# A hybrid decoder layer on one core: VectorE's other work behind the score masks, GpSimd scaling in halves, block stores in the order of their read

## The chip, the cores and the metric

The kernel runs on one core of one Trainium2 chip. The metric is the device time of one execution in microseconds (us), as the median of several runs. A profile of one execution comes from the hardware profiler.

## The reference

One inference step of a decoder layer with d = 1024, for one prompt of 512 tokens and eight sample requests of 4 tokens each, which share all weights (so 544 columns per matmul row block). A SwiGLU feed-forward part (half a step), a layer norm, then a mixer, a layer norm, a second feed-forward part and a last norm. Only the mixer is touched here:

```python
proj = x @ p["w_in"]                       # 1024 -> 3328
ps_mix = ps + p["mu_shift"] * (prev - ps)  # token shift, gives r, k, v, wd, ad, gd
o, wkv_new = wkv7_recurrence(r_h, w_h, k_h, v_h, kk, a_h, wkv0)
#   S <- S diag(w) + (S (-kk)) (kk*a)^T + v k^T ;  o = S r      per head, per token
u = c_c * c_h
z = cw[0] * u_full[:, 0:T] + cw[1] * ... + cw[2] * ...
y_conv = c_b * z
mix = jnp.concatenate([y_rwkv, y_conv], axis=-1) @ p["w_out"]
```

Half of the mixer is the recurrence of 8 heads of 64, the other half a short convolution of three taps over 512 channels, with a gate before and behind it.

## The kernel before

**Weights.** Matmuls run on a split format: ScalarE writes the high half of a weight (L147), VectorE the rest, the low half (L148, 128x1024 a time). Weights come through a ring of `raw` tiles and a ring of `hl` tiles (`ring`, L109 to L115); a `raw` tile is loaded by SP's queue and is free again when both halves are made. `mm3` (L159) does three matmuls per block: high by high, high by low part of the input, low by high. Only the third reads the low half. It yields after every six.

**Order.** A scheduler lists the instructions of each engine; while `pinned[0]` is set, TensorE's follow the program. `bg` is a queue of generators with background work (projections and convolutions); `take(ns)` draws so many nanoseconds of it into the program, `need(p, n)` draws until pair p is that far. `tc.issue_after(ins)` puts whatever is emitted under it behind `ins` in the order list, on its engine.

**The recurrence.** The 512 tokens are cut into 8 chunks of 64, and the sample's tokens make a ninth (index 8). Heads go in four pairs (`Pair`, L884 to L988), one head on each half of the partitions. For each pair: gates, squares and decays, `prep` (VectorE multiplies keys and queries by decay products, L931 to L944), then `scores`, where TensorE runs pinned. `masked(0, 4)` and `masked(4, 4)` make the products AO of chunks 0 to 7, and VectorE multiplies them by masks into SC (L955, four times 128x512). Two DMAs per pair store the parts of SC that the elimination needs to `Ad` in DRAM, GpSimd scales `bkb` (L962), and at `yield 1` the main loop puts in `FILL["s"]` = 600 ns of background work, which is one step of a convolution: six matmuls. Then `masked(8, 1)` for the sample, the transposes of `vt` and `bkb`, whose results ScalarE moves to UV (L977) and BK (L984), and the `Pn` products (L988). A PSUM pool `sm` has 5 banks, `big` (tile name `mm`) 3. After the scores of pair p, the rest of pair p + 1 (`own_b`: decays, prep, the vt projection) is drawn.

**Convolutions.** `conv` (L810) makes c, then h (multiplied to u), then the taps on VectorE (L806), then the gate, one tile `zc` for all of it.

**After the pairs.** `elim` (L992) reads `Ad` to AT, inverts all 32x32 triangles in 31 pairs of VectorE steps (L1006, L1008), stores the result De and its transpose to `Dd`, reads them as DM and XT, and joins the blocks in two rounds of small matmuls, with copies of XT on VectorE and ScalarE (L1036). `sample` (L1127) treats the ninth chunk while `elim` runs. `chain` (L1049) goes through the chunks one after another: `values` makes W (L1066), `solve` multiplies by XT, then `update` and `outputs`.

Of the kernel before, what the change touches and what calls it, by code (L numbers as in the profile page):

```python
# [62 lines left out]
def body(ctx: ExitStack, tc: tile.TileContext, xT, gu1, wd1, win, wo_c, wo_r, gu2, wd2, lora, vec, cst,  # L63
# [746 lines left out]
    def conv(i):  # L810
        u = cvp.tile([P, 2 + TP + 6 * NSEQ], F32, name="cu")
        zc = cvp.tile([P, T], F32, name="zc")
        us = u[:, 514:].rearrange("p (b t) -> p b t", t=6)
# [65 lines left out]
    POOL.memset(cm[:, 512:576:4], 0.0)  # L879
    Ad = dr.tile([2, 32, 65, 64], F32, name="Ad")  # L880
    Dd = [dr.tile([2, 32, 2, 32, 32], F32, name=f"Dd{i}") for i in range(2)]
    SEG = ((0, 256, 0), (256, 576, 1))

    class Pair:  # L884
# [61 lines left out]
        def scores(self):  # L946
            p, bkb, vf = self.p, self.bkb, vfs[self.p]
            def masked(a0c, n):
                qs = (sm(), sm())
                for c in range(n):  # L950
                    for par, q in enumerate(qs):
                        PE.matmul(q[:, c * P:c * P + P], bkb[R(par), a0c + c, :, :],
                                  AO[R(par), 0:p + 2:p + 1, a0c + c, :] if n > 1 else AR8[R(par), p, :, :], start=True, stop=True)
                for par, q in enumerate(qs):
                    DVE.tensor_tensor(SC[:, p, par, a0c:a0c + n, :], q[:, :P * n].rearrange("p (c t) -> p c t", c=n),  # L955
                                      (msk if n > 1 else msks)[:, None, :].to_broadcast([P, n, P]), op=OP.mult)

            masked(0, 4)
            masked(4, 4)
            for par in range(2):  # L960
                dma(Ad[par].rearrange("(c d) s t -> d s c t", d=4)[p, 0:64], SC[R(par), p, par, 0:8, 0:64])
            POOL.tensor_tensor(bkb[:, 0:8], bkb[:, 0:8], Pe[:, p, :, None, None].to_broadcast([P, 8, 2, 64]), op=OP.mult)  # L962
            yield 1
            masked(8, 1)
            for a0c, n in ((0, 5), (5, 4)):
                qs = (big(), sm())
# [25 lines left out]
    def elim(XT, DM):  # L992
# [4 lines left out]
        tm = ep.tile([P, 256], F32, name="tm")  # L997
        dma(AT, bass.AP(tensor=Ad.tensor, offset=Ad.offset, ap=[[2080, P], [64, 32], [1, 32]]))
        POOL.memset(De, 0.0)
# [49 lines left out]
    def chain(XT, tl):  # L1049
# [10 lines left out]
        def values(g, c):  # L1060
            q = sm()
            for pl, par in PP:
                p, r = 2 * g + pl, slice(0, P) if c else R(1 - par)
                PE.matmul(q[R(par), pl * 64:pl * 64 + 64], SC[r, p, par, c, 0:64], UV[r, p, par, c, :], start=True, stop=True)
            W[g] = tl([P, 2, 64], F32, name=f"W{g}")
            ACT.activation(W[g], v2(q), AF.Copy)  # L1066
# [35 lines left out]
        def outputs(g, c):  # L1102
# [3 lines left out]
            if c % 4 == 3:  # L1106
                ACT.activation(O[:, 2 * g:2 * g + 2, c - 3:c + 1, :],
                               qo[g].rearrange("p (c d t) -> p d c t", c=4, d=2), AF.Copy)

        for c in range(8):  # L1110
            if c % 4 == 0:
                qo[:] = big(), big()
            values(0, c)
            if c:
                reads(0, c)
            values(1, c)
            solve(0, c)
            if c:
                reads(1, c)
            solve(1, c)  # L1120
            yield 0
            for g in range(2):
                update(g, c)
                outputs(g, c)
            yield 0

    def sample(cp):  # L1127
        tl = cp.tile
        S0 = tl([P, 4, NSEQ, 64], F32, name="S0")
        dma(S0, s0)  # L1130
        WT = tl([P, 4, 32], F32, name="WT")
        SI = tl([P, 4, 2, 64], F32, name="SI")
        D8 = tl([P, 4, 32], F32, name="D8")
        X8 = tl([P, 4, 64], F32, name="X8")
        UP = tl([P, 4, 64], F32, name="UP")
        HR = [slice(96 * par, 96 * par + 32) for par in range(2)]
# [19 lines left out]
        for rnd in range(3):  # L1156
# [12 lines left out]
            reads(rnd)  # L1169
            yield 0  # L1170
        reads(3)
        for par in range(2):
            pr = R(par)
# [5 lines left out]
        for pl, par in PLP:  # L1179
            PE.matmul(q[R(par), pl * 64:pl * 64 + 64], SC[:, pl, par, 8, 0:64], SI[:, pl, par, :], start=True, stop=True)  # L1180
        W = tl([P, 4, 64], F32, name="W")
        ACT.activation(W, v4(q), AF.Copy)
# [4 lines left out]
        DVE.tensor_copy(UV[R(0), :, 0, 8, :], v4(q[0], R(0)))  # L1187
        ACT.copy(UV[R(1), :, 1, 8, :], v4(q[1], R(1)))
        DVE.tensor_tensor(UP, UV[:, :, 0, 8, :], UV[:, :, 1, 8, :], op=OP.add)
        uxs = [tl([P, NSEQ, 64], F32, name="ux", bufs=4) for _ in range(4)]  # L1190
# [77 lines left out]
    POOL.tensor_copy(T12[:, T:576], T12[:, 512:T])  # L1268
    ACT.activation(sgd, sgd, AF.Sigmoid)
    pairs[0].gates()  # L1270
    pairs[0].square()
    wget(4)
    wget(5)
    pairs[0].decays()
    pairs[0].prep()
    drain(project(4, 8, 0, vfs[0]), project(4, 8, 1, vfs[0]))
    bg.append(convs)
    for p in range(4):
# [6 lines left out]
        for _ in pairs[p].scores():  # L1285
            take(FILL["s"])
        pinned[0] = False
        if p < 3:
            bg.appendleft(own_b(p + 1))
            need(p + 1, 2)  # L1290
            take(FILL["p0"])
    pst.close()
# [25 lines left out]
    next(el)  # L1318
    drain(conv3)
    for _ in el:  # L1320
        pass
# [11 lines left out]
    cst0 = ExitStack()  # L1333
    cp = pool(cst0, "chain")
    for _ in chain(XT, cp.tile):
        pass
# [48 lines left out]

    f2.s1[0] = s1
    f2.open()
    lnq = f2.open_lnq()
# [87 lines left out]
```

## Time and profile before

| what | value |
|---|---|
| median of three runs | 1082.21 us (1079.39 to 1083.17) |
| the profiled execution | 1080.19 us, its span in the profile 1078.4 us |
| TensorE busy | 1054.3 us, 98% of the span |
| VectorE busy | 833.0 us, 77% |
| ScalarE busy | 564.3 us, 52% |
| GpSimd busy | 206.4 us, 19% |
| TensorE's granted clock, mean | 0.991 |

PE is TensorE's matmuls, DVE is VectorE, ACT is ScalarE, POOL is GpSimd, SP the engine that issues most DMAs. In a timeline a bracket tells how long the engine sat idle before the instruction and what released it. A granted clock of 1.00 is 2.4 GHz, 0.50 is 1.2 GHz. The mixer's pairs lie at about 405 to 530 us, elimination and sample at 530 to 598, the chain from there to about 626.

### The profile page before, as it was taken

Reading aid. Unit: us, or ns where it says so; the run is one execution under the profiler, and the core shown is the slowest. Engines: PE = TensorE matmul, PEld = TensorE weight load, DVE = VectorE, ACT = ScalarE, POOL = GpSimd, SP = SyncE. Lnnn points to the kernel's source line nnn. Section 1 sums busy time; section 2 is a strip of 40 time slices with the busy share of each in tenths; the row PEclk is TensorE's granted clock in tenths of the full one; section 3 lists DMA queues with packets and bytes.
Section 4 is the critical chain, followed back from the end, with each engine's and each line's share of the span. In section 5 each row is a group of like instructions: output and inputs, shape, how many; then the busy total and the mean of one; then the engine's idle time right before and its main releaser. Section 6 shows DMA issues by size and latency. Waiting matters only on the chain.

```text
span 1078.4 us, 22059 instructions
## 1 busy us (share of the span) xinstructions
PE 1054.3 (98%) x8960; PEld 1021.0 (95%) x8960; DVE 833.0 (77%) x1528; ACT 564.3 (52%) x1015; POOL 206.4 (19%) x296
## 2 busy tenths in 40 slices
PE   9999999999999999999999999999999999999996
PEld 8999999999999998888989899999999999999995
DVE  7798888889775857787588578878889888887755
ACT  6655565555552567555312464466554655545524
POOL 0122230312200023343220410010313122130000
PEclk9999999999999999999989999999999999999998
DMA  8568595866854231222616631424957759496302
GB/s 295 129 125 191 124 216 134 177 158 145 197 122 147 77 116 40 69 52 87 153 59 200 237 104 40 138 59 89 213 145 164 178 125 225 105 211 138 104 1 84
DMA packets 82887, 144.78 MB, mean 134 GB/s; under 512 B 20448, under 2 KB 44384, under 8 KB 82528
## 3 DMA queue, kind: packets, MB, share of 16 engines
q1 hardware_dynamic: 55584, 107.19, 30.7%
q0 software_dynamic: 27200, 36.18, 21.7%
q8 instruction: 70, 1.15, 0.4%
q14 instruction: 33, 0.27, 0.1%
HBM read 124.37 MB, written 10.06 MB: 125 GB/s over the span
## 4 chain that ended last, share of the span: by engine, by line
PE 79%; DVE 9%; DMA 6%; ACT 3%; issue 2%; SPq 0%; POOL 0%; ACTq 0%; DVEq 0%; POOLq 0%
PE mm L76 50%; PE sm L76 29%; DVE hl L148 2%; DMA z<-sv 2%; DMA z<-cpb 1%; ACT hl L147 1%; DVE De L1008 1%; DMA raw<-in_gu 1%; DVE SC L955 1%; DVE tm L1006 1%; DVE hhl L152 1%; DMA raw<-in_wd 1%; DMA DM<-Dd 1%; DMA z<-in_xT 0%; DVE z L610 0%
## 5 line engine op out<-in xcount | busy, mean ns | idle before, releaser
L76 PE MATMUL mm<-xhl,hl 128*128 128x288 f32 (+2 forms) x2640 | 362.8, 293 | 3.5 <-DVE hl L148 2.3
L76 PEld LDWEIGHTS mm<-xhl,hl 128*128 128x128 f32 x2640 | 343.6, 189 | 11.2 <-DVE hl L148 2.5
L148 DVE TENSOR_TENSOR hl<-raw,hl 128x1024 fp32r<-128x1024 f32 (+3 forms) x224 | 262.0, 1175 | 69.1 <-ACT hl L147 68.3
L147 ACT ACTIVATE hl<-raw 128x1024 fp32r<-128x1024 f32 (+3 forms) x224 | 224.4, 1012 | 91.6 <-DVE raw L487 31.3
L76 PE MATMUL sm<-xhl,hl 128*128 128x272 f32 (+1 forms) x1392 | 193.8, 289 | 0.3 <-DVE xhl L152 0.3
L76 PEld LDWEIGHTS sm<-xhl,hl 128*128 128x128 f32 x1392 | 182.3, 189 | 1.5 <-ACT xhl L151 0.6
L76 PE MATMUL mm<-tv,hl 128*128 128x272 f32 x864 | 121.3, 289 | 1.9 <-ACT cpb L587 1.8
L76 PE MATMUL mm<-hhl,hl 128*128 128x272 f32 (+2 forms) x792 | 119.2, 294 | 0.1
L76 PEld LDWEIGHTS mm<-tv,hl 128*128 128x128 f32 x864 | 113.3, 188 | 3.0 <-ACT cpb L587 2.3
L76 PEld LDWEIGHTS mm<-hhl,hl 128*128 128x128 f32 x792 | 105.9, 188 | 5.1 <-ACT sv L626 1.5
L76 PE MATMUL sm<-hhl,hl 128*128 128x272 f32 (+2 forms) x792 | 109.6, 288 | 0.0
L76 PEld LDWEIGHTS sm<-hhl,hl 128*128 128x128 f32 x792 | 103.0, 188 | 0.5
L493 POOL DMA_DIRECT2D raw<-in_gu x36 | 43.5, 1209 | 256.2 <-DVE cpb L583 81.4
L499 POOL DMA_DIRECT2D raw<-in_wd x32 | 39.3, 1469 | 269.2 <-DVE hlb L152 235.6
L76 PE MATMUL mm<-tv,hlb 128*128 128x272 f32 x432 | 61.1, 291 | 0.8 <-ACT cpb L590 0.8
L76 PEld LDWEIGHTS mm<-tv,hlb 128*128 128x128 f32 x432 | 56.4, 188 | 2.3 <-ACT cpb L590 2.2
L151 ACT ACTIVATE hhl<-sv 128x272 fp32r<-128x272 f32 (+1 forms) x52 | 26.0, 512 | 30.8 <-DVE sv L350 12.1
L152 DVE TENSOR_TENSOR hlb<-raw,hlb 128x512 fp32r<-128x512 f32 x52 | 35.7, 687 | 4.2 <-ACT hlb L151 4.2
L151 ACT ACTIVATE hhl<-hk 128x272 fp32r<-128x272 f32 (+1 forms) x48 | 24.2, 504 | 27.5 <-DVE hk L557 12.9
L218 ACT ACTIVATE lnq<-z 128x512 f32<-128x512 f32 (+1 forms) x24 | 14.9, 654 | 41.5 <-DVE z L217 41.5
L487 DVE TENSOR_TENSOR raw<-raw 128x512 f32<-128x512 f32 x52 | 35.8, 689 | 1.0
L76 PE MATMUL mm<-hhl,hlb 128*128 128x272 f32 (+2 forms) x264 | 36.4, 288 | 0.0
(294 smaller groups left out, 1325.9 us busy)
## 6 DMA issues: line engine op xcount, KB each, us to landing
raw<-in_gu SPq DMA_DIRECT2D x84, 512.0 KB, 4.6
raw<-in_gu POOLq DMA_DIRECT2D x36, 512.0 KB, 6.2
raw<-in_wd SPq DMA_DIRECT2D x32, 512.0 KB, 4.7
raw<-in_win SPq DMA_DIRECT2D x26, 512.0 KB, 3.6
raw<-in_wd POOLq DMA_DIRECT2D x32, 256.0 KB, 6.0
raw<-in_wd SPq DMA_DIRECT2D x16, 384.0 KB, 3.1
z<-cpb POOLq DMA_DIRECT2D x16, 272.0 KB, 9.0
z<-sv POOLq DMA_DIRECT2D x16, 272.0 KB, 7.3
```

The lines of the kernel that those rows point to most:

```text
L76: ins = f(*args, **kw)
L147: ACT.activation(hl[:, 0, a:b], raw[:, a:b], AF.Copy)
L148: DVE.tensor_tensor(hl[:, 1, a:b], raw[:, a:b], hl[:, 0, a:b].bitcast(F32), op=OP.subtract)
L151: ACT.activation(hi, x, AF.Copy)
L152: DVE.tensor_tensor(lo, x, hi.bitcast(F32), op=OP.subtract)
L218: sq = ACT.activation(qq, zz, AF.Square)
L487: DVE.tensor_tensor(y[:, :, 0], y[:, :, 1], a[:, :, 1], op=OP.add)
L493: POOL.dma_start(x.rearrange("p (s c) -> p s c", s=2), bass.AP(tensor=a11.tensor, offset=a11.offset, ap=[[2 * D, P], [P * 2 * D, 2], [1, 5 ...
L499: POOL.dma_start(four(x)[:, i], bass.AP(tensor=a11.tensor, offset=a11.offset, ap=[[DFF, P], [P * DFF, 2], [1, 256]]), accum_op=OP.add)
L955: DVE.tensor_tensor(SC[:, p, par, a0c:a0c + n, :], q[:, :P * n].rearrange("p (c t) -> p c t", c=n), (msk if n > 1 else msks)[:, None, :].t ...
L1006: DVE.tensor_tensor(tv, AT[:, k, k + 1:32, None].to_broadcast([P, n, k + 1]), De[:, k, None, 0:k + 1].to_broadcast([P, n, k + 1]), op=OP.mult)
L1008: DVE.tensor_tensor(De[:, k + 1:32, 0:k + 1], De[:, k + 1:32, 0:k + 1], tv, op=OP.add)
```

## The change

It does eight things, all between the first projections of the mixer and the start of the chain:

- In the main loop, all background work that is drawn during and after a pair's scores stands behind `pairs[p].mk`, the last mask emitted so far (at `yield 1` the fourth).
- GpSimd scales `bkb` in two halves, each right after its four chunks; the second bank of `masked(8, 1)` comes from `big`, and the transposes go in groups of 4 and 5 chunks rather than 5 and 4.
- `Ad` is laid out as the blocks that the elimination reads: four stores of 32x8x32 in place of two of 64x8x64 for each pair, and a contiguous read.
- `zc` gets two buffers.
- Two weights are fetched ahead of pair 0's gates, and four steps of the convolutions and one more fetch run ahead of pair 0's vt projection.
- `values(0, 0)` and `values(1, 0)` of the chain are emitted ahead of the last rounds of `elim`; W of chunk 0 uses AR8's space.
- `sample` uses two tile names for two purposes each, and asks for 600 ns of filler in its second and third round.
- The counter of the `raw` ring is set to 0 ahead of the second feed-forward part.

```diff
-        zc = cvp.tile([P, T], F32, name="zc")
+        zc = cvp.tile([P, T], F32, name="zc", bufs=2)
...
-    Ad = dr.tile([2, 32, 65, 64], F32, name="Ad")
+    Ad = dr.tile([2, 32, 2, 32, 32], F32, name="Ad")
...
             def masked(a0c, n):
-                qs = (sm(), sm())
+                qs = (sm(), sm() if n > 1 else big())
...
-                    DVE.tensor_tensor(SC[:, p, par, a0c:a0c + n, :], q[:, :P * n].rearrange("p (c t) -> p c t", c=n),
+                    self.mk = DVE.tensor_tensor(SC[:, p, par, a0c:a0c + n, :], q[:, :P * n].rearrange("p (c t) -> p c t", c=n),
...
-            masked(0, 4)
-            masked(4, 4)
+            for c in (0, 4):
+                masked(c, 4)
+                POOL.tensor_tensor(bkb[:, c:c + 4], bkb[:, c:c + 4], Pv[:, c:c + 4].to_broadcast([P, 4, 2, 64]), op=OP.mult)
             for par in range(2):
-                dma(Ad[par].rearrange("(c d) s t -> d s c t", d=4)[p, 0:64], SC[R(par), p, par, 0:8, 0:64])
-            POOL.tensor_tensor(bkb[:, 0:8], bkb[:, 0:8], Pe[:, p, :, None, None].to_broadcast([P, 8, 2, 64]), op=OP.mult)
+                for b in range(2):
+                    dma(Ad[par, :, b].rearrange("(c d) s t -> d s c t", d=4)[p],
+                        SC[64 * par + 32 * b:64 * par + 32 * b + 32, p, par, 0:8, 32 * b:32 * b + 32])
             yield 1
             masked(8, 1)
-            for a0c, n in ((0, 5), (5, 4)):
+            for a0c, n in ((0, 4), (4, 5)):
...
-        dma(AT, bass.AP(tensor=Ad.tensor, offset=Ad.offset, ap=[[2080, P], [64, 32], [1, 32]]))
+        dma(AT, Ad.rearrange("a c b s t -> (a c b) s t"))
...
-            W[g] = tl([P, 2, 64], F32, name=f"W{g}")
+            W[g] = tl([P, 2, 64], F32, name=f"W{g}") if c else AR8[:, g]
...
+        values(0, 0)
+        values(1, 0)
+        yield 0
...
+    wget(4)
+    wget(5)
     pairs[0].gates()
     pairs[0].square()
-    wget(4)
-    wget(5)
     pairs[0].decays()
     pairs[0].prep()
+    drain(islice(convs, 4))
+    wget(6)
     drain(project(4, 8, 0, vfs[0]), project(4, 8, 1, vfs[0]))
...
         for _ in pairs[p].scores():
-            take(FILL["s"])
+            with tc.issue_after(pairs[p].mk.ins):
+                take(FILL["s"])
         pinned[0] = False
         if p < 3:
             bg.appendleft(own_b(p + 1))
-            need(p + 1, 2)
-            take(FILL["p0"])
+            with tc.issue_after(pairs[p].mk.ins):
+                need(p + 1, 2)
+                take(FILL["p0"])
...
     drain(conv3)
+    cpool = [None]
+    ch = chain(XT, lambda *a, **k: cpool[0].tile(*a, **k))
+    next(ch)
     for _ in el:
         pass
```

What this does to the order is seen at three places, all in pair 1. First VectorE from the end of pair 1's projections through its masks. `SC` lines are masks, `zc` lines of L806 the taps of convolution 0, `hl_` lines low halves of weights, `kq`, `AO` and `AR8` lines pair 2's prep. Before:

```order
L938 TENSOR_TENSOR AO_4712<-r_4313,Pi_5553 128x512
L939 TENSOR_TENSOR AR8_4713<-r_4313,Pi_5553 128x64
L148 TENSOR_TENSOR hl_5678<-raw_5677,hl_5678 128x1024
L955 TENSOR_TENSOR SC_4719<-sm_5456,cs_4710 128x512
L955 TENSOR_TENSOR SC_4719<-sm_5457,cs_4710 128x512
L955 TENSOR_TENSOR SC_4719<-sm_5468,cs_4710 128x512
L955 TENSOR_TENSOR SC_4719<-sm_5469,cs_4710 128x512
L955 TENSOR_TENSOR SC_4719<-sm_5489,cs_4710 128x128
L955 TENSOR_TENSOR SC_4719<-sm_5490,cs_4710 128x128
L932 SCALAR_TENSOR_TENSOR AO_4712<-kq_5404,Pi_5553 128x512
L936 TENSOR_TENSOR kq_5404<-kq_5404,a_5279 128x576
```

And now:

```order
L957 TENSOR_TENSOR SC_4719<-sm_5479,cs_4710 128x512
L957 TENSOR_TENSOR SC_4719<-sm_5480,cs_4710 128x512
L957 TENSOR_TENSOR SC_4719<-sm_5492,cs_4710 128x512
L957 TENSOR_TENSOR SC_4719<-sm_5493,cs_4710 128x512
L806 SCALAR_TENSOR_TENSOR zc_4506<-cu_4505,vc_66,zc_4506 128x512
L806 SCALAR_TENSOR_TENSOR zc_4506<-cu_4505,vc_66,zc_4506 128x32
L806 SCALAR_TENSOR_TENSOR zc_4506<-cu_4505,vc_66,zc_4506 128x512
L806 SCALAR_TENSOR_TENSOR zc_4506<-cu_4505,vc_66,zc_4506 128x32
L148 TENSOR_TENSOR hl_5518<-raw_5517,hl_5518 128x1024
L957 TENSOR_TENSOR SC_4719<-sm_5529,cs_4710 128x128
L957 TENSOR_TENSOR SC_4719<-mm_5530,cs_4710 128x128
L931 SCALAR_TENSOR_TENSOR kq_5426<-k0_4314,vc_66,kq_5426 128x576
```

The two lines of prep and the split that stood ahead of the masks have gone behind them, and between the fourth mask and the two narrow ones there are now the taps and one split.

TensorE at the same place, from the end of the AO products: the fill of six matmuls (`xhl` by a weight), chunk 8 (`AR8`) and the first transposes. Before:

```order
L76 MATMUL sm_5469<-AO_4712,bkb_5144 128x128
L76 MATMUL mm_5449<-xhl_68,hl_5248 128x288 x6
L76 MATMUL sm_5489<-AR8_4713,bkb_5144 128x128
L76 MATMUL sm_5490<-AR8_4713,bkb_5144 128x128
```

And now:

```order
L76 MATMUL sm_5493<-AO_4712,bkb_5178 128x128
L76 MATMUL mm_5522<-xhl_68,hl_5518 128x256 x6
L76 MATMUL sm_5529<-AR8_4713,bkb_5178 128x128
L76 MATMUL mm_5530<-AR8_4713,bkb_5178 128x128
L76 MATMUL mm_5535<-cs_4710,vt_4297 64x64
```

The fill was the middle of a product whose weight hl_5248 had been in use for 30 matmuls; now it is the first use of hl_5518, whose low half is the ninth line of VectorE's list above.

ScalarE now, from the tap that it does itself to the first evictions of pair 1 (`UV` and `BK`):

```order
L147 ACTIVATE hl_5622<-raw_5621 128x1024
L804 ACTIVATE zc_4506<-cu_4505,vc_66 128x512
L804 ACTIVATE zc_4506<-cu_4505,vc_66 128x32
L981 ACTIVATE UV_4721<-mm_5535 64x256
L981 ACTIVATE UV_4721<-sm_5536 64x256
L147 ACTIVATE hl_5749<-raw_5748 128x1024
L988 ACTIVATE BK_4720<-sm_5547 128x4x64
L988 ACTIVATE BK_4720<-sm_5548 128x4x64
L981 ACTIVATE UV_4721<-mm_5559 64x320
L981 ACTIVATE UV_4721<-sm_5560 64x320
L988 ACTIVATE BK_4720<-sm_5573 128x5x64
```

Before, no split stood among pair 1's evictions; now the one of hl_5749 stands between the first of UV and the first of BK.

## Rows read from the trace of the kernel before

**Rows 1.** The page: busy time by engine, and DMA issues (median us to landing).
```profile
PE 1054.3 (98%) x8960; PEld 1021.0 (95%) x8960; DVE 833.0 (77%) x1528; ACT 564.3 (52%) x1015; POOL 206.4 (19%) x296
...
raw<-in_win SPq DMA_DIRECT2D x26, 512.0 KB, 3.6
```

**Rows 2.** Windows, the four pairs: us; busy of PE, PEld, DVE, ACT, POOL; PEclk, DMA.
```profile
400.00:540.00 140.00, 134.32 (x1164) 124.14 (x1164) 97.23 (x181) 80.02 (x165) 50.17 (x111) 0.99 0.29 83
```

**Rows 3.** PE's timeline in pair 0: start, us, instruction, [idle before, releaser].
```profile
424.27 2.86 PE L76 MATMUL mm<-xhl,hl 128*128 128x256 f32 x22 [2.32 <-DVE hl L148]
...
434.15 1.06 PE L76 MATMUL mm<-xhl,hl 128*128 128x288 f32 x6
...
436.07 0.49 PE L76 MATMUL sm<-AR,bkb 64*128 64x128 f32 x2 [0.45 <-DVE SC L955]
...
440.77 1.24 PE L76 MATMUL sm<-Pn,cs 128*128 128x256 f32 x4 [0.82 <-ACT BK L984]
441.60 1.11 PE L76 MATMUL mm<-xhl,hl 128*128 128x256 f32 x6
```

**Rows 4.** PE's timeline in pair 1: fill, first BK transpose, next projection.
```profile
468.21 1.06 PE L76 MATMUL mm<-xhl,hl 128*128 128x288 f32 x6
...
471.41 0.24 PE L76 MATMUL sm<-cs,bkb 64*128 64x64 f32 x1 [0.15 <-DVE SC L955]
...
473.74 1.46 PE L76 MATMUL mm<-xhl,hl 128*128 128x256 f32 x9
```

**Rows 5.** DVE's timeline: pair 1's split and masks, convolution taps, pair 3's split.
```profile
468.24 1.22 DVE L148 TENSOR_TENSOR hl<-raw,hl 128x1024 fp32r<-128x1024 f32 x1
469.38 2.88 DVE L955 TENSOR_TENSOR SC<-sm,cs 128x512 f32<-128x512 f32 x6
...
484.87 1.73 DVE L806 SCALAR_TENSOR_TENSOR zc<-cu,vc,zc 128x512 f32<-128x512 f32 x4
...
524.28 1.23 DVE L148 TENSOR_TENSOR hl<-raw,hl 128x1024 fp32r<-128x1024 f32 x1 [3.66 <-ACT hl L147]
```

**Rows 6.** Groups by line and form, DVE, 405 to 530: busy us, mean ns.
```profile
L936 DVE TENSOR_TENSOR kq<-kq,a 128x576 f32<-128x576 f32 x4 | 3.4, 849 | 0.1
...
L955 DVE TENSOR_TENSOR SC<-sm,cs 128x128 f32<-128x128 f32 x8 | 1.9, 281 | 0.0
...
L939 DVE TENSOR_TENSOR AR<-r,Pi 128x64 f32<-128x64 f32 x4 | 0.9, 218 | 0.0
```

**Rows 7.** ACT's timeline: a split, BK evictions in pair 1, W of the chain.
```profile
466.34 1.07 ACT L147 ACTIVATE hl<-raw 128x1024 fp32r<-128x1024 f32 x1
...
472.42 0.77 ACT L984 ACTIVATE BK<-sm 128x320 f32<-128x320 f32 x2 [0.24 <-PE sm L76]
...
598.78 0.45 ACT L1066 ACTIVATE W<-sm 128x128 f32<-128x128 f32 x2
```

**Rows 8.** Windows with a low clock (columns as in rows 2).
```profile
504.00:510.00 6.00, 5.59 (x51) 4.58 (x52) 5.56 (x11) 3.61 (x9) 2.86 (x3) 0.72 0.52 134
542.00:550.00 8.00, 8.00 (x106) 7.66 (x104) 3.77 (x14) 0.59 (x3) 0.00 (x0) 0.57 0.01 2
```

**Rows 9.** POOL's timeline: the scaling of bkb in pairs 1 and 3.
```profile
468.40 2.82 POOL L962 TENSOR_TENSOR bkb<-bkb,Pe 128x1024 f32<-128x1024 f32 x1
...
524.97 2.30 POOL L962 TENSOR_TENSOR bkb<-bkb,Pe 128x1024 f32<-128x1024 f32 x1 [0.79 <-PE sm L76]
```

**Rows 10.** PE's timeline behind the elimination: a convolution, the chain's first solve.
```profile
583.83 0.92 PE L76 MATMUL mm<-xhl,hl 128*128 128x288 f32 x5 [1.22 <-ACT zc L838]
...
599.89 0.99 PE L76 MATMUL sm<-W,XT 64*64 64x64 f32 x16 [1.14 <-ACT W L1066]
```

**Rows 11.** DVE's timeline: copies of XT ahead of the chain.
```profile
599.12 1.27 DVE L1036 COPY XT<-sm 32x512 f32<-32x512 f32 x2
```

**Rows 12.** DMA issues, 526 to 593: KB each, median us to landing.
```profile
AT<-Ad SPq DMA_DIRECT2D x1, 512.0 KB, 7.1
Dd<-De SPq DMA_DIRECT2D x1, 512.0 KB, 2.7
```

More of the change, by code (lines that the diff above doesn't have):

```diff
@@ L947, in scores @@
             p, bkb, vf = self.p, self.bkb, vfs[self.p]
+            Pv = Pe[:, p, :, None, None]
             def masked(a0c, n):
-                qs = (sm(), sm())
+                qs = (sm(), sm() if n > 1 else big())
                 for c in range(n):
@@ L1112, in chain @@
                 qo[:] = big(), big()
-            values(0, c)
             if c:
+                values(0, c)
                 reads(0, c)
-            values(1, c)
+                values(1, c)
             solve(0, c)
@@ L1130, in sample @@
         dma(S0, s0)
-        WT = tl([P, 4, 32], F32, name="WT")
         SI = tl([P, 4, 2, 64], F32, name="SI")
-        D8 = tl([P, 4, 32], F32, name="D8")
+        D8 = tl([P, 4, 32], F32, name="WT")
         X8 = tl([P, 4, 64], F32, name="X8")
-        UP = tl([P, 4, 64], F32, name="UP")
         HR = [slice(96 * par, 96 * par + 32) for par in range(2)]
@@ L1169, in sample @@
             reads(rnd)
-            yield 0
+            yield 600 if rnd else 0
         reads(3)
+        WT = tl([P, 4, 32], F32, name="WT")
         for par in range(2):
@@ L1180, in sample @@
             PE.matmul(q[R(par), pl * 64:pl * 64 + 64], SC[:, pl, par, 8, 0:64], SI[:, pl, par, :], start=True, stop=True)
-        W = tl([P, 4, 64], F32, name="W")
+        W = tl([P, 4, 64], F32, name="UP")
         ACT.activation(W, v4(q), AF.Copy)
@@ L1188, in sample @@
         ACT.copy(UV[R(1), :, 1, 8, :], v4(q[1], R(1)))
+        UP = tl([P, 4, 64], F32, name="UP")
         DVE.tensor_tensor(UP, UV[:, :, 0, 8, :], UV[:, :, 1, 8, :], op=OP.add)
@@ L1333, in body @@
     cst0 = ExitStack()
-    cp = pool(cst0, "chain")
-    for _ in chain(XT, cp.tile):
+    cpool[0] = pool(cst0, "chain")
+    for _ in ch:
         pass
@@ L1386, in body @@
     f2.s1[0] = s1
+    wstate["raw"] = 0
     f2.open()
```

## The prediction

> **What bounds the kernel now.** I read the page first, then windows, then the timelines of single engines. On the page TensorE is busy 98% of the span [rows 1]: the kernel is bound by matmuls, and only idle PE time or a lower clock can be won back. The changed code runs between about 400 and 605 us; ahead of it and from the chain's second round on, the order of every engine is the same as before. From 400 to 540, the stretch of the four pairs, PE is busy 134.32 of 140 us, so 5.7 us of idle time lie there [rows 2]. The timeline names the larger gaps. In pair 0 PE waits 2.32 us for a weight split on VectorE (L148), 0.45 for a mask (L955) and 0.82 for an eviction of BK (L984) [rows 3]; in pair 1 the waits are short (0.15 at 471.41) [rows 4]. Later come 1.22 us for the single zc buffer and 1.14 ahead of the chain [rows 10]. The clock gives the rest: from 504 to 510, behind pair 2's short waits and while PE does 64-column transposes, it reads 0.72, a stretch at the lower level (1.2 GHz) that costs 0.28 x 6 = 1.7 us; from 542 to 550, after the sample's 8-column matmuls, it reads 0.57, which costs 0.43 x 8 = 3.4 us [rows 8].
>
> **The change part by part.**
>
> *Filler behind the masks, pair 1.* This is the largest term. In scores PE runs in program order: the AO products, six filler matmuls of a convolution, chunk 8, the transposes, the Pn products. A split weight has a high half (ScalarE, L147) and a low half (VectorE, L148), and every third matmul needs the low half. Before, the fill used a weight split long ago and started at 468.21 without a wait [rows 4]; call that moment A. Now the fill is the first user of hl_5518, and the order lists show VectorE's half of it behind four masks and four convolution taps. The first mask can start about 0.6 us before A, when half of the AO products are done. Six masks take 2.88, less two narrow ones of 0.28 makes 2.3 for the four; the taps take 1.73, the split 1.22 [rows 5, 6]. The low half is there at A - 0.6 + 2.3 + 1.73 + 1.22 = A + 4.6; the fill asks for it at A + 0.25. That is a wait of **4.4 us** with no counterpart before. It goes on late: ScalarE now has the split of hl_5749 ahead of BK's evictions, and its raw tile can only be loaded when hl_5518's split has given up a slot of the ring (A + 4.6). A load lands in 3.6 us [rows 1], the split takes 1.07, a BK eviction 0.4 [rows 7], Pn's products some 0.8. The next projection starts at about A + 10.5, where before it was 473.74, A + 5.5 [rows 4]; the matmuls in between differ by 0.1 us. The upper end is thus +5. The lower is +1.4, if BK's evictions wait for nothing and the shorter transposes win back 2 us. I take **+4.2**, nearer the upper end, since each piece has a row.
>
> *The same in pairs 2 and 3.* In pair 2 one L825 (about 0.7, as the taps' wide halves) and the split of hl_5950 stand behind the masks: A - 0.6 + 2.3 + 0.7 + 1.22 = A + 3.6, a wait of some 3.3 us; the old waits and slack behind them give back about 2.8. The low half of the next vt weight stands behind the whole of prep and adds 1.0. Together **+1.5** (0 to +3). In pair 3 the fill's weight is early and a short old wait goes: -0.3.
>
> *Pair 0.* Four early steps of the convolutions run ahead of the vt projection, so matmuls take the place of the 2.32 us, and the waits of 0.45 and 0.82 go: -3.59 [rows 3]. What is late next is the projection of pair 1's vt: its low half stands behind six masks (2.88), six operations of prep, from 0.22 (L939) to 0.85 (L936), 3.5 together, and itself (1.22) [rows 5, 6]. With 0.45 of waiting for chunk 8 that is 8.0 us from the first mask, A - 0.6 + 8.0 = A + 7.4, where PE would come to it at 441.60 - 434.15 - 1.27 = A + 6.2 [rows 3]. So 1.2 to 2 come back: **-2.0** (-3.6 to -1.4).
>
> *The clock.* A wait of 4 us is longer than any that PE has here now; the spells I can price follow shorter ones [rows 8]. Pair 2's spell probably stays and one like it comes in pair 1: **+1.7** (0 to +3.4, the price of the sample's).
>
> *GpSimd scaling halved.* L962 took 2.82 us in pair 1, where a VectorE split (468.24, 1.22 long) ran beside it for its first 1.06, and 2.30 in pair 3, where the split (524.28, 1.23) lay over its first 0.54: 1.76 without it, both times [rows 5, 9]. So a half takes about 0.9, and the second is over at A + 0.9. In pair 1 the BK transposes started (471.41, wait 0.15) just when the scaling had ended (468.40 + 2.82) [rows 4, 9]: that wait goes, and is in the terms above. The Trainium skill's page "SBUF — State Buffer", section "Who interferes with whom", says that a VectorE operation with two SBUF inputs and a GpSimd read exclude each other for a whole instruction; the two rows agree with it. By that rule the taps could stand behind a half, up to 0.9 us; by the rows the half is over before the masks are, at A + 1.7, and nothing is added.
>
> *Blocks stored as read.* Each pair stores four times 32 KB in runs of 128 bytes in place of twice 128 KB in runs of 256: as many runs, half the bytes, on SP's queue, where only weight loads wait. The read of AT took 7.1 us in pieces of 128 bytes; the same 512 KB in one piece per partition took 2.7 (Dd<-De) [rows 12], and 3.6 for a weight [rows 1]. So AT lands 3.5 to 4.4 us earlier against pair 3's end, and the elimination may start sooner by at most that. PE is then full of convolution matmuls, so it only makes DM earlier: 0 (-1.4 to +1). The Trainium skill's page "DMA: Bandwidth & Descriptors", Specifications, puts full rate at runs of 512 bytes and up, which speaks against the shorter runs of the stores. By it a store would cost as long as before for half the bytes (an estimate), and the elimination would gain 1 us less; no sum changes.
>
> *zc in two buffers.* The wait of 1.22 us at 583.83 goes [rows 10]: **-1.2** (0 to -1.2).
>
> *Chain's first values ahead of a round.* PE's 1.14 us at 599.89 is put down to W, but ScalarE had W ready at 598.78 + 0.45, while VectorE copied XT from 599.12 on, two copies in 1.27 [rows 7, 10, 11]. The copies stay where they are, behind zc, a split and L825: 0 (-0.4 to 0). The ring counter set to 0 stands at a multiple of the ring's five slots there: 0. Sample's shared names and its filler: 0 (-1 to +1).
>
> Sum: 4.2 + 1.5 - 0.3 - 2.0 + 1.7 - 1.2 = **+3.9 us**. On the profiled execution's 1080.19 that is 1084.1; that execution lies 2.0 under the median of 1082.21, and against the median I forecast **1086**.
>
> **The rivals.** *Faster.* The masks come first, so chunk 8 and the transposes never wait, and the fill's low half is there in time. Then the pairs' 5.7, the spell of 1.7 and zc's 1.2 go: 1082.2 - 8.6 = **1074**. It decides at one point: hl_5518's low half must be done by A + 0.25. For it: this is where PE's idle time of today lies [rows 2, 3]. Against it: VectorE works in order, and its own rows add up to A + 4.6 [rows 5, 6]. 0.20. *No change.* The wait in pair 1 is half as long (+2), ScalarE's split holds nobody back, pair 2 costs 0.5 and no new spell comes: -2.0 + 2 + 0.5 - 0.3 - 1.2 = -1, about **1081** (1080 to 1083). 0.17. *Slower still.* Both long waits bring the longer spell, 3.4 each in place of 1.7 together: +3.9 + 5.1 = +9, up to **1091**, or only one does, 1088. 0.15. *The forecast*: 0.48.
>
> **How the numbers follow.** About 0.3%, or 3.2 us, is what a measurement of this kernel can tell from no change. The forecast's own range is 1083 to 1089; some two thirds of it lie over 1085.4, which with "slower still" makes 0.45 for slower. The other third, "no change" and a little of the faster case make 0.38; faster keeps 0.17. The range reaches down to 1077, which takes in a faster case that comes out half, and up to 1091.
>
> **What would show it.** In pair 1 of the changed kernel PE should wait about 4.4 us inside the six filler matmuls, with L148 as releaser, and again about 2 us for BK; pair 2 some 3 us; in pair 0 there is no wait of 2.32. The clock falls under 1 in pair 1. AT lands in 4 us or less, and the wait at 583.83 is gone. I am wrong if pair 1 has no wait over 1 us, if the wait is there but later work takes it up (then a wait after 530 us must have shrunk by as much), or if the clock holds in the pairs.

## The result and the profile after

The changed kernel takes **1092.99 us** (median of 5 runs, 1091.37 to 1093.83); the kernel before took 1083.17 in the same series (5 runs, 1079.39 to 1085.6). The ratio is 1.0089, with an interval from 1.0064 to 1.0115: slower by about 10 us. The forecast had the sign, 1086 us, and was 7 us short; the time lies 2 us above the range.

The page of the changed kernel, its busy times and the group of matmuls out of bank `mm` (busy us, mean ns | idle before, and what ended most of it):

```profile
PE 1059.7 (97%) x8960; PEld 1024.8 (94%) x8960; DVE 833.4 (76%) x1528; ACT 563.3 (52%) x1015; POOL 200.1 (18%) x300
...
L76 PE MATMUL mm<-xhl,hl 128*128 128x288 f32 (+2 forms) x2640 | 368.3, 296 | 10.2 <-DVE hl L148 9.8
```

The profiled execution's span is 1091.2 us, 12.8 over that of before. PE is busy for 5.4 us more with the same 8960 matmuls, which is a lower clock, and idle for 7.4 us more (1091.2 - 1059.7 = 31.5, before 1078.4 - 1054.3 = 24.1). Of the idle time 9.8 us now wait for L148. PE's timeline of the changed kernel shows where (start, us, instruction, idle before it and its releaser):

```profile
430.59 1.24 PE L76 MATMUL sm<-kq,cs 128*128 128x256 f32 x4 [1.11 <-ACT kq L903]
...
445.90 9.79 PE L76 MATMUL mm<-xhl,hl 128*128 128x256 f32 x64 [2.24 <-DVE hl L148]
...
473.03 0.50 PE L76 MATMUL mm<-xhl,hl 128*128 128x256 f32 x2
477.84 1.22 PE L76 MATMUL mm<-xhl,hl 128*128 128x256 f32 x4 [4.30 <-DVE hl L148]
...
482.79 2.29 PE L76 MATMUL sm<-Pn,cs 128*128 128x256 f32 x4 [0.42 <-ACT BK L988]
484.41 5.77 PE L76 MATMUL mm<-xhl,hl 128*128 128x256 f32 x36
...
517.39 1.22 PE L76 MATMUL mm<-xhl,hl 128*128 128x256 f32 x4 [3.23 <-DVE hl L148]
...
605.70 0.22 PE L76 MATMUL sm<-DM,SC 32*32 32x32 f32 x2 [0.97 <-DMA DM<-Dd]
...
614.30 0.77 PE L76 MATMUL sm<-AR,XT 64*64 64x64 f32 x16 [0.76 <-ACT XT L1040]
```

The filler of pair 1 starts at 473.03, does its two matmuls that need only the high half, and stands for 4.30 us; before, the fill went through [rows 4]. Pair 2 repeats it with 3.23. VectorE's timeline in pair 1 has the reason in three lines, four masks, the taps and the split, one behind the other:

```profile
472.53 2.48 DVE L957 TENSOR_TENSOR SC<-sm,cs 128x512 f32<-128x512 f32 x4
474.92 1.73 DVE L806 SCALAR_TENSOR_TENSOR zc<-cu,vc,zc 128x512 f32<-128x512 f32 x4
476.57 1.22 DVE L148 TENSOR_TENSOR hl<-raw,hl 128x1024 fp32r<-128x1024 f32 x1
```

The clock is the other half. In the windows of the changed kernel (us; busy time of PE, PEld, DVE, ACT, POOL; granted clock, DMA) four spells at the lower level stand where the kernel before had three:

```profile
444.00:450.00 6.00, 4.10 (x23) 4.10 (x24) 5.99 (x10) 0.46 (x1) 0.94 (x3) 0.72 0.31 90
476.00:488.00 12.00, 9.74 (x69) 8.42 (x70) 9.93 (x18) 4.43 (x10) 1.87 (x4) 0.57 0.32 92
516.00:526.00 10.00, 8.61 (x66) 7.35 (x67) 7.32 (x15) 4.43 (x10) 2.84 (x4) 0.66 0.34 93
558.00:570.00 12.00, 12.00 (x130) 11.21 (x129) 7.65 (x20) 1.19 (x4) 0.28 (x2) 0.57 0.18 59
```

Three follow the waits of 2.24, 4.30 and 3.23 us, the fourth the sample's small matmuls. Busy time by one minus the clock gives 1.1 + 4.2 + 2.9 + 5.2 = 13.4 us of lost full-speed time. Before it was 1.6 + 3.4 [rows 8], and 1.7 in a third spell from 600 to 606, which the changed kernel does not have: 6.7.

### The profile page after: what moved, and what is told of

It is laid out like the page before. It is cut to its first block, busy times and chain, and to the rows that moved or that the text cites. A ratio compares the mean times of both kernels' runs of the same rounds, so it can differ in the third digit from the quotient of the medians.

```text
span 1091.2 us, 22054 instructions
## 1 busy us (share of the span) xinstructions
PE 1059.7 (97%) x8960; PEld 1024.8 (94%) x8960; DVE 833.4 (76%) x1528; ACT 563.3 (52%) x1015; POOL 200.1 (18%) x300
## 4 chain that ended last, share of the span: by engine, by line
PE 81%; DVE 9%; DMA 4%; ACT 3%; issue 2%; SPq 0%; POOL 0%; ACTq 0%; DVEq 0%; POOLq 0%
PE mm L76 52%; PE sm L76 29%; DVE hl L148 2%; DMA z<-cpb 1%; DMA z<-sv 1%; DMA raw<-in_gu 1%; DVE SC L957 1%; DVE hhl L152 1%; DMA raw<-in_wd 1%; ACT hl L147 1%; DVE De L1012 1%; DVE tm L1010 0%; DMA z<-in_xT 0%; DMA DM<-Dd 0%; DVE z L610 0%
## 5 line engine op out<-in xcount | busy, mean ns | idle before, releaser
L76 PE MATMUL mm<-xhl,hl 128*128 128x288 f32 (+2 forms) x2640 | 368.3, 296 | 10.2 <-DVE hl L148 9.8
L76 PEld LDWEIGHTS mm<-xhl,hl 128*128 128x128 f32 x2640 | 347.9, 192 | 18.7 <-DVE hl L148 10.4
L148 DVE TENSOR_TENSOR hl<-raw,hl 128x1024 fp32r<-128x1024 f32 (+3 forms) x224 | 263.3, 1179 | 66.2 <-ACT hl L147 65.2
```

What stands on the lines that cost most here:

```text
L76: ins = f(*args, **kw)
L148: DVE.tensor_tensor(hl[:, 1, a:b], raw[:, a:b], hl[:, 0, a:b].bitcast(F32), op=OP.subtract)
```

## The experiments

In all runs the kernel before ran beside on the same chip, with medians of 1082.3 to 1083.0 us in the four series of the experiments. First the times, then what each run was for.

| run | median us | ratio to before, interval |
|---|---|---|
| the change | 1093.0 | 1.0089 (1.0064 to 1.0115) |
| e1, filler not tied behind the masks | 1087.3 | 1.0050 (1.0028 to 1.0072) |
| e2, no early convolution steps | 1100.8 | 1.0168 (1.0144 to 1.0193) |
| e3, no ties at all | 1087.1 | 1.0040 (1.0020 to 1.0060) |
| e4, sample without filler | 1093.3 | 1.0100 (1.0068 to 1.0132) |
| e5, the rest alone (no ties, no early steps) | 1088.9 | 1.0051 (1.0031 to 1.0071) |
| e6, the ties alone, in the kernel before | 1101.6 | 1.0165 (1.0138 to 1.0192) |
| e7, the change, low halves left out of the ties | **1081.0** | 0.9979 (0.9960 to 0.9999) |
| e8, more matmuls during the waits | 1107.5 | 1.0215 (1.0185 to 1.0245) |
| e9, the same with the order kept | 1100.8 | 1.0167 (1.0139 to 1.0195) |
| e10, e5 with the old banks and groups | 1094.0 | 1.0094 (1.0057 to 1.0132) |
| e11, e7 with the old banks and groups | 1082.0 | 0.9991 (0.9965 to 1.0017) |
| e12, e5 with the scaling in one piece | 1083.9 | 1.0007 (0.9994 to 1.0019) |

**Which tie costs (e1, e2, e3).** e1 takes the tie off the filler:

```diff
-            with tc.issue_after(pairs[p].mk.ins):
-                take(FILL["s"])
+            take(FILL["s"])
```

> The changed kernel, but the filler drawn inside the scores is not tied behind the masks (the rest of the next pair still is). Theory A, that TensorE waits in the filler for a low half of a weight that stands behind masks and taps, and that each such wait is followed by a spell at the lower clock: the waits of 4.30 and 3.23 us in pairs 1 and 2 fall below 0.5 us, the spells behind them (about 4.1 and 3.1 us of lost time) go, and the time falls by 11 to 14 us, to 1079 to 1082 us. Rival B, that the prep of the next pair behind the masks is what costs (its split comes late, as in the wait of 2.24 us of pair 0): less than 4 us come back, 1089 us or more.

The waits in the fillers were gone, but only 5.7 us came back, half of theory A's. In e1's PE timeline the next split is late instead, a wait of 1.27 us for L148 at 481.66, and pair 0's 2.24 stays (2.25). The profiled execution, at 1082.3 us, is the fastest of e1's ten, and the clock reads 1.00 behind both waits; what made the others slower, up to 1093.5, no trace shows. e2 leaves both ties and drops `drain(islice(convs, 4))` and `wget(6)`:

> The changed kernel without the four convolution steps and the one fetch ahead of pair 0's vt projection; both ties behind the masks stay. Theory A: the filler then falls into the middle of a product again, whose weight is long split, so the waits of 4.30 and 3.23 us go although everything is still tied behind the masks; the 2.32 us of pair 0 come back: 1081 to 1085 us. Rival B: the next pair's prep is as late as in the changed kernel, and 1090 us or more remain.

A miss: it became slower by 8 us. The fillers of pairs 1 and 2 are in mid product here, as expected, and have no wait; others came in their place. PE's timeline of e2:

```profile
481.83 18.95 PE L76 MATMUL mm<-xhl,hl 128*128 128x256 f32 x140 [3.75 <-DVE hl L148]
...
519.53 13.20 PE L76 MATMUL mm<-xhl,hl 128*128 128x256 f32 x92 [4.92 <-DVE hl L148]
...
539.63 1.17 PE L76 MATMUL mm<-xhl,hl 128*128 128x256 f32 x4 [4.50 <-DVE hl L148]
```

The first two are in the next pair's vt projection, whose low half stands behind the masks and nearly the whole of that pair's prep; the third is in pair 3's filler. So theory A was too narrow. e3 takes both ties off:

> The changed kernel with neither tie behind the masks; everything else of the change stays. Theory A: as without the filler's tie, and the 2.24 us wait of pair 0 goes too with most of its spell: 1077 to 1081 us, below the kernel before or level with it. Rival C, that the rest of the change (four-and-five transposes, early convolution steps, block stores, sample's filler) costs by itself: 1085 us or more.

1087.1 us, on rival C's side. Its largest wait is again for L148, 3.35 us at 483.81, behind prep, which the scheduler now places there of its own accord; the masks are late as well, with waits of 1.52 and 1.35 us at 474.07 and 514.05. From these three I formed **theory D**: what costs is VectorE's queue order alone; wherever a low half stands behind masks, taps or prep, PE waits for it, and ties and early steps only decide which one it is.

**Theory D (e5, e6, e7).** e6 is the kernel before with both ties and nothing else:

> The kernel before with both ties behind the masks and nothing else of the change. Theory D: the convolution weight of the next stretch is split only behind the whole prep of the next pair, as in the run without early steps, so TensorE waits 3 to 5 us for L148 behind pairs 1 and 2 and in pair 3's filler, in all 12 to 16 us of waits: 1095 to 1101 us, slower than the whole change. Rival: the ties do harm only together with the early steps' shift of the filler, 1085 us or less.

1101.6 us, as theory D had it, with waits for L148 of 2.32, 0.68, 3.64, 4.83 and 4.47 us, 15.9 in all, and one of 3.95 us for the single `zc` at 604.35. The ties alone are worse than the whole change; its early steps hide part of the harm, as e2 has shown, and its second `zc` buffer has no such wait. VectorE's timeline of e6, pair 1: between the last mask and the split lie 8.2 us, prep nearly all of it.

```profile
471.08 2.88 DVE L955 TENSOR_TENSOR SC<-sm,cs 128x512 f32<-128x512 f32 x6
473.88 0.81 DVE L931 SCALAR_TENSOR_TENSOR kq<-k,vc,kq 128x576 f32<-128x576 f32 x1
...
480.60 1.52 DVE L942 TENSOR_TENSOR bkb<-k,Pn 64x576 f32<-64x576 f32 x2
482.15 1.23 DVE L148 TENSOR_TENSOR hl<-raw,hl 128x1024 fp32r<-128x1024 f32 x1
```

e7 is the test proper. It ties everything behind the masks but the low halves of weights (`lows` collects the names of L148's instructions):

```diff
+    def behind(mk, f):
+        traced = nc.cur_bb.bb.instructions
+        n = len(traced)
+        f()
...
+        for i in traced[n:]:
+            if i.engine == mk.ins.engine and i.name not in lows:
+                tc.add_manual_dep(i, mk.ins.name, info, reason="behind")
...
-            with tc.issue_after(pairs[p].mk.ins):
-                take(FILL["s"])
+            behind(pairs[p].mk, lambda: take(FILL["s"]))
...
```

> The whole change, but the low halves of weights (L148) are left out of both ties; masks still come ahead of taps, prep and everything else on VectorE. Theory D: the waits for L148 of 4.30 and 3.23 us are gone or under 1 us, and with them the spells at the lower clock in pairs 1 and 2; 9 to 13 us come back, 1080 to 1084 us. Rival E, that the taps and the prep behind the masks are late for TensorE even so (their products feed the next pair's scores and the gate): 1087 us or more, with waits for other lines in place of L148.

1081.0 us: 12 us came back, and the kernel is level with the one before or a little faster (0.9979, interval 0.9960 to 0.9999). No wait for L148 is left between 405 and 660 us. Windows of e7 through the pairs:

```profile
440.00:490.00 50.00, 49.13 (x425) 45.40 (x425) 39.43 (x73) 31.07 (x63) 17.22 (x39) 1.00 0.21 62
490.00:530.00 40.00, 39.08 (x369) 36.23 (x368) 27.68 (x52) 19.65 (x44) 14.08 (x34) 1.00 0.36 101
```

PE is idle for 1.8 us in 90, and the clock is at its full level throughout. Over all executions the mean granted clock was 0.983 to 0.987 in the change and 0.987 to 0.995 in e7. Masks, taps and prep are tied as in the change, so rival E falls: they are not late for PE, only the low halves were.

**The clock by itself (e8, e9).** To part the waits from the clock, e8 gives PE something to do in the waits of pairs 1 and 2: 40 and 30 additional matmuls ahead of the filler, in a part of its bank that nothing reads.

```diff
-        q = big()
+        q = big(); [PE.matmul(q[:, 288:512], xhl[:, 0, 0, 0:P], xhl[:, 0, 1, 0:224], start=True, stop=True) for _ in range(extra.pop() if extra else 0)]
...
-                take(FILL["s"])
+                take(extra.append((0, 40, 30, 0)[p]) or FILL["s"])
```

> The whole change, and in pairs 1 and 2 TensorE runs 40 and 30 additional matmuls of 224 columns ahead of the filler, into an unused part of the filler's bank, for about the 4.3 and 3.2 us in which it waited. They add work and leave every wait where it is. Theory F, that the spells at the lower clock follow from the idle time and are a cost of their own: the clock stays at 1.0 in pairs 1 and 2, and the 4.1 and 3.1 us lost there come back, 1085 to 1088 us. Rival: the transposes behind the wait bring the clock down anyway, or VectorE is what the stretch waits for and nothing comes back: 1091 us or more.

It told nothing of the clock: the scheduler, which counts the additional matmuls, put another split ahead of chunk 8's masks, and PE waited 5.45 and 4.50 us for those. e9 ties that split, and ScalarE's half of it, so that the order through the scores is the change's:

> As the run with additional matmuls during the waits (40 in pair 1, 30 in pair 2), whose scheduling had put another split ahead of chunk 8's masks; here VectorE's and ScalarE's order through the scores of pairs 1 and 2 is kept as in the whole change. Theory F: between the AO products and the end of pair 1's transposes the clock stays at 1.0, so from the AO products to the Pn products pair 1 takes about 10 us in place of 11.7 (471.05 to 482.79) and pair 2 about 9 in place of 10.2, and the spells of 4.1 and 3.1 us are gone; a later split may still be waited for, 1086 to 1091 us in all. Rival: the clock falls in the transposes behind the wait although TensorE was busy before, and the stretches stay at 11.7 and 10.2 us.

The stretches came out as theory F said: from the AO to the Pn products pair 1 takes 9.9 us (470.84 to 480.71) against 11.7 (471.05 to 482.79), pair 2 8.8 against 10.2. PE's timeline of e9, pair 1:

```profile
470.84 2.06 PE L76 MATMUL sm<-AO,bkb 64*128 64x128 f32 x32
...
480.71 1.24 PE L76 MATMUL sm<-Pn,cs 128*128 128x256 f32 x4
```

Windows of e9 over the two stretches, with the clock at 1.00:

```profile
471.00:481.00 10.00, 9.75 (x120) 9.06 (x121) 8.71 (x19) 3.14 (x8) 2.73 (x5) 1.00 0.28 66
515.40:524.20 8.80, 8.55 (x110) 7.80 (x109) 7.38 (x15) 3.02 (x7) 3.49 (x7) 1.00 0.47 139
```

The same stretches in the change, 471 to 483 and 511.7 to 522, read 0.72 and 0.77:

```profile
471.00:483.00 12.00, 7.28 (x81) 6.15 (x81) 9.76 (x22) 4.27 (x9) 3.58 (x8) 0.72 0.22 55
511.70:522.00 10.30, 7.07 (x81) 6.06 (x80) 8.13 (x18) 3.37 (x8) 3.58 (x7) 0.77 0.41 119
```

So in these two stretches it was the idle time that brought the clock down, and the clock cost 1.9 and 1.4 us up to the Pn products, on top of the wait. The total of e9, 1100.8, is a miss against 1086 to 1091: new waits of 1.72 and 2.95 us came right behind pair 1 (an eviction, and L148 again), and a spell with them. It says nothing about the sum.

**The sample's filler (e4).** `yield 600 if rnd else 0` becomes `yield 0`.

> The changed kernel, but the sample asks for no filler between its rounds, as before the change. Theory A: the spell at the lower clock behind the sample's small matmuls shrinks from about 5.1 us of lost time to the 3.4 us of the kernel before; 1 to 2 us come back, 1091 to 1092 us. Rival: filler or not, the clock falls for the same stretch, and nothing that can be told from 1093 us changes.

The spell became shorter, 560 to 568 with some 3.4 us of loss in place of 5.2, and the time did not move (1093.3). So the rival's time holds. Whether the filler lengthens the spell stays open: e5 and e7 keep the filler, and their profiled executions lose 3.4 us there too.

**What the rest costs (e5, e10, e12).** e5 has neither ties nor early steps:

> Neither the ties behind the masks nor the early convolution steps; the block stores, the two zc buffers, the halved scaling, the four-and-five transposes, the chain's early values and the sample's filler stay. Theory D, formed on the runs so far: what costs is VectorE's queue order alone, where a low half of a weight (L148) stands behind masks, taps or prep; here the fill is again in mid product and the splits stand ahead of the masks, so no L148 wait over 2.5 us, the old 2.32 of pair 0 stays, zc's 1.22 goes: 1080 to 1083 us, level with the kernel before. Rival C, that the other parts cost some 5 us by themselves, as the 1087 us without ties might mean: 1085 us or more.

1088.9 us: no wait for L148 over 2.30, but the time is rival C's. In pairs 1 and 2 the first vt transposes wait 1.04 and 1.02 us for a mask. PE's timeline of e5, pair 1:

```profile
471.73 0.24 PE L76 MATMUL sm<-cs,vt 64*64 64x64 f32 x1 [1.04 <-DVE SC L957]
```

e10 undoes the banks and groups in e5:

> The run of the rest alone (neither ties nor early steps, 1088.9 us), with chunk 8's second bank from the five and the transposes in groups of five and four again, as in the kernel before. Theory G, that the banks cost: the waits of some 1.0 us of the first vt transposes on a mask in pairs 1 and 2 go back to 0.4, and 2 to 4 us come back, 1085 to 1087 us or less. Rival: they are small change, and the time stays within 1.5 us of 1088.9; then the sample's filler, the stores or the chain's early values hold the loss.

1094.0, and both guesses missed; with four executions its interval overlaps that of e5, so it need not be slower. The wait is now at chunk 8 and 1.28 long, since the second bank from `sm` must wait for the first mask. So the masks themselves are late. The lines of e5 show why, GpSimd's timeline first:

```profile
468.96 3.02 POOL L962 TENSOR_TENSOR bkb<-bkb,Pe 128x512 f32<-128x512 f32 x2
```

and VectorE's, at the same moment:

```profile
469.00 2.07 DVE L148 TENSOR_TENSOR hl<-raw,hl 128x1024 fp32r<-128x1024 f32 x1
471.00 2.67 DVE L957 TENSOR_TENSOR SC<-sm,cs 128x512 f32<-128x512 f32 x5
```

The first half of the scaling starts 0.04 us ahead of the split, and the split takes 2.07 us in place of 1.22. In the kernel before it was the other way round: the split started first, and the scaling took longer [rows 5, 9]. e12 puts the scaling back in one piece and changes nothing else; VectorE's and TensorE's orders are the same as in e5.

> The run of the rest alone (1088.9 us) with GpSimd's scaling in one piece behind all eight chunks again; nothing else differs, and VectorE's and TensorE's orders are the same. In the run of the rest alone the first half started 0.04 us ahead of VectorE's split, and the split took 2.07 us in place of 1.22. Theory H, that the halves block the split and so the masks: the split takes 1.22 us again, TensorE's waits of about 1.0 us on masks in pairs 1 and 2 fall to 0.5 or less, and 2 to 5 us come back, 1084 to 1087 us. Rival: the waits go but they were covered, and 1088 to 1089 us stay; then the loss lies in the sample, the stores or the chain's early values.

1083.9 us: 5 us came back, and the split takes 1.22 us again. VectorE's timeline of e12 in pair 1:

```profile
471.93 1.22 DVE L148 TENSOR_TENSOR hl<-raw,hl 128x1024 fp32r<-128x1024 f32 x1
473.07 2.48 DVE L957 TENSOR_TENSOR SC<-sm,cs 128x512 f32<-128x512 f32 x4
```

The first vt transposes wait 0.19, and the BK transposes 0.74, until the whole scaling is done. PE's timeline of e12:

```profile
473.81 0.24 PE L76 MATMUL sm<-cs,vt 64*64 64x64 f32 x1 [0.19 <-DVE SC L957]
```

So halving the scaling costs some 5 us in e5, where a half starts just ahead of the split that the masks wait for. How the 5 us divide into waits and clock is not shown. The whole change does not pay that: in pairs 1 and 2 its masks come first, have one operand in PSUM, and the halves run beside them in 2.04 us for both. Nor does e7, although a split stands just ahead of the masks there too: the halves start only behind it. VectorE's and GpSimd's timelines of e7, pair 1:

```profile
468.83 1.22 DVE L148 TENSOR_TENSOR hl<-raw,hl 128x1024 fp32r<-128x1024 f32 x1
...
470.20 2.03 POOL L973 TENSOR_TENSOR bkb<-bkb,Pe 128x512 f32<-128x512 f32 x2
```

**Banks with the low halves free (e11).**

> The whole change with the low halves left out of the ties (1081.0 us), and with the old banks and groups of five and four. Theory G: another 1 to 3 us less, 1078 to 1080 us, the fastest of all. Rival: with the masks first on VectorE the banks come free early enough either way, and the time stays within 1 us of 1081.

1082.0 us, within the intervals of e7: the rival. e7 stays the fastest kernel that was run.

## Why the prediction was wrong

The mechanism was right, and sizes were off. The step that failed is *The clock*, "+1.7 (0 to +3.4)": the full-speed time lost to the lower clock rose by 6.7 us (13.4 against 6.7). That makes 5.0 of the 8.9 us by which the span outgrew the sum (12.8 against 3.9). Another 1.7 stand ahead of the changed stretch, and about 2 are waits that the other terms had too small, in pairs 0 and 2 above all. I take the parts in turn, and place them by when the pairs' AO products start. These starts were 432.16, 466.23, 499.94 and 522.79 before, and are 435.64, 471.05, 511.68 and 539.07 now. The convolution matmuls that the change has already done by then (3.33, 2.59, 2.59 and 2.95 us, counted in the order lists) are taken off, and the chain's first solve is 14.4 us later (599.89 to 614.30) with the same work done.

- **Start of the changed stretch.** The first gate products stand 1.7 us later (407.64 against 405.91) with the same order ahead of them; 1.0 of it is a longer wait for `cpb` at 289.04, long before (1.38 in place of 0.41). It is part of the 12.8 in span, but not of the change.
- **Pair 0**, forecast -2.0. From the gates to pair 1's AO products the sum is +0.5. The 2.32 us wait is gone, as are 0.45 and 0.82, but the wait for pair 1's vt split is 2.24, somewhat over the 1.2 to 2 foreseen, a wait of 1.11 for kq at 430.59 was not foreseen (all runs with the early steps have it, none without), and the spell behind the 2.24 costs 1.1.
- **Pair 1**, forecast +4.2 and 1.7 of clock, 5.9 in all. Measured +6.9. The low half came at A + 4.76 (477.79, A being 473.03) where the sum of VectorE's rows had A + 4.6, and the wait was 4.30 where it had 4.4. BK's evictions held PE back by 0.42 only, not by about 2: the `raw` load went out at 477.85, as foreseen, and landed in 3.5 us while PE was still busy with the fill, chunk 8 and the transposes at the slower clock. The clock cost 4.2 in place of 1.7, so what was too much for BK and too little for the clock nearly met: the next projection starts at A + 11.4, not at A + 10.5.
- **Pair 2**, forecast +1.5. Measured +4.2. The wait was 3.23 where 3.3 were foreseen; the spell behind it is 2.9 us where the old one cost 1.6, and little of the 2.8 that the forecast had for old waits and slack was given back.
- **Pair 3, elimination and sample**, forecast -1.5. Measured +1.1. zc's wait at 583.83 is gone, but a spell of 5.2 us in place of 3.4 lies over the sample, and at the end PE waits 0.97 and 0.47 us for DM, which no longer has convolution matmuls in front of it for long enough. AT did not land in 4 us but in 5.5. S0's load of 1 MB is issued 1.2 us ahead of it, where it was 2.1 before; whether that holds AT up was not tested. The DMA issues of the read and the stores in the changed kernel, 520 to 565 (KB each, us to landing):

```profile
AT<-Ad SPq DMA_DIRECT2D x1, 512.0 KB, 5.5
Ad<-SC SPq DMA_DIRECT2D x4, 32.0 KB, 1.7
```

  The elimination started 1.1 us after AT had landed and took 44.6 us (552.36 to 597.0) where it had taken 42.7, as VectorE waited for the sample's slow products in between. The four stores of a pair land in 1.7 us each where the two larger ones took 2.7, so the shorter runs show no cost here.
- **Chain.** PE's 1.14 us of before read 0.76 for XT and 0.20: 0.2 us, as foreseen nothing much. The spell of 600 to 606 did not come, -1.6.

The clock's parts were priced with the rows of short waits, although the forecast itself said that a wait of 4 us is longer than any seen. "Slower still", with 0.15 and up to 1091 us, was the rival that came nearest, through a wider door: not two long spells but four, one of them where I had forecast a gain (pair 0) and one where I had forecast nothing (the sample). What the change gained in waits of its own it did gain, and what it lost is shown by e7: with the low halves out of the ties, and every other part as it is, the loss is gone.

A second step failed that did not show in the sum: under *GpSimd scaling halved* I compared the halves with the masks and the taps of the change only and set the cost to nothing. For the change that is so. It depends on which starts first, a half or a split that stands ahead of the masks, as e5, e7 and e12 show.

What stays open: e5 and e10 differ by 5 us though their waits differ by less than 1; e10's profile shows five spells at the lower clock where e5's has three, but that is the slowest of e10's four against the second fastest of e5's ten, and it also waits 2.08 us for `cpb` at 992.19, far from the changed stretch. No run here separates what each is worth. The runs of e1, e3, e5 and e11 also scatter by 7 to 12 us from one to the next, and only the profiled run of each has a trace. The mean clock goes some way with it (in e11 0.994 at 1078.5 us and 0.984 at 1090.3).

## What to carry to other kernels

A tie that sends "everything else" behind an urgent operation also sends what the bounding engine needs next. Before adding one, list for each instruction that it delays who waits for it and when, and leave those out: here one exception for the weight splits is worth 12 us. And a wait on the matmul engine is to be priced twice, once for itself and once for the slower clock that can come behind it. In pairs 1 and 2 of the change that second price was about as large as the first; in e2 it was less, 1.2, 1.3 and 2.8 us behind waits of 3.75, 4.92 and 4.50 (by the windows 480 to 486, 518 to 524 and 538 to 548).

## What was not expected of the hardware

- **The same wait does not always bring the lower clock.** Behind waits of 2.24, 4.30 and 3.23 us in the changed kernel the clock was at the lower level for some 3, 10 and 7 us. The page "TensorE: Matmul & The Clock Gate" of the Trainium skill, section "HAM oscillation", describes matmuls after DMA waits that run at half clock; the traces agree in kind (windows at 0.50 behind every one of the three), and e9 shows the cause by filling two of the waits. But the wait of about 2.3 us in pair 0, which eleven of the fourteen traces have (2.24 to 2.32), brought the spell in eight of them and none in three: before, e1 and e5. All fifteen longer waits, of 2.95 to 5.45 us, brought it. Windows behind that wait, first in the kernel before, where it ends at 424.27, then in the changed kernel, where it ends at 445.90:

```profile
426.00:428.00 2.00, 2.00 (x15) 1.77 (x13) 1.62 (x3) 1.63 (x4) 1.45 (x3) 1.00 0.49 199
...
446.00:448.00 2.00, 2.00 (x10) 2.00 (x11) 2.00 (x6) 0.00 (x0) 0.00 (x0) 0.50 0.49 102
```

  So a spell that one trace shows behind a wait of this size is no fixed price, and one that it does not show is no proof of none. What decides between them, no run here shows.
- **Which of two engines starts first decides who is held up.** Split first (the kernel before): split 1.22 us, the whole scaling 2.82 in place of 1.76, which is worked out from two overlaps. Half scaling first, by 0.04 us (e5): split 2.07, the two halves 3.02 in place of 2.04. The Trainium skill's page "SBUF — State Buffer", section "Who interferes with whom", calls the port pair that the two share an exclusive lock, on which a VectorE operation with two SBUF inputs and a GpSimd read contend, and says that the order of issue decides who is blocked; the kernel before and e5 agree with it: the split was held up for 2.07 - 1.22 = 0.85 us, and a half by itself takes about 1.0 (2.04 for two in the change).
